# Group A's queries and gates projected with features on partitions, and the queries' norm moved into the scale of the exponential

## The chip, the cores and the metric

The kernel runs on one core of a Trainium2 chip. The metric is the time of one execution on the device in microseconds (us), the median over runs. Engines are named as in the profile: PE (TensorE, the matmuls) with PEld (its weight loads), DVE (VectorE), ACT (ScalarE), POOL (GpSimd) and SP (SyncE, which issues most transfers). Products run on float32r operands; where full precision is wanted, a tensor is split into a high and a low part and three products (high by high, high by low, low by high) are summed.

## The reference

Two layers of a trunk with 512 latent tokens and 256 context tokens, 1024 wide. A layer norms and modulates the tokens, projects them to the queries, keys and values of three groups of heads (A, B, C, eight heads of 64 features each) and to a gate, attends, multiplies by the gate and projects back. The second layer computes the latents alone. Group A, which the change touches:

```python
def rmsnorm(x, w):
    xf = x.astype(jnp.float32)
    y = xf * lax.rsqrt(jnp.mean(xf * xf, axis=-1, keepdims=True) + EPS)
    return y.astype(x.dtype) * w

def apply_rope(x, cos, sin):
    x1, x2 = jnp.split(x, 2, axis=-1)
    ...
    return jnp.concatenate([x1 * c - x2 * s, x1 * s + x2 * c], axis=-1)

def global_gqa(q, k, v, qc, kc, vc, cos, sin, qn, kn, need_ctx):
    scale = HEAD_DIM ** -0.5
    q = apply_rope(rmsnorm(heads(q, N_HEADS_A), qn), cos, sin) * scale
    k = apply_rope(rmsnorm(heads(k, N_KV_A), kn), cos, sin)
    ...
    def block(qi):
        s = jnp.einsum('bqhgd,bkhd->bhgqk', qi, k_all)
        p = softmax_f32(s, v_all.dtype)
        return jnp.einsum('bhgqk,bkhd->bqhgd', p, v_all)

# in layer():
    ux = jnp.concatenate([ya, yb, yc_], axis=-1) * jax.nn.silu(px[9])
```

The context's queries of A are normed and scaled too, not rotated, and read the context's keys only.

## The kernel before

**Layout.** The normed tokens stand with features on partitions, as `hh` and `hl` (high and low), eight tiles of 128 features: `hL` for the 512 latents, `hC` for the 256 context tokens. There are two ways to project. `proj_t` (products at L341) makes the tokens the stationary operand and streams 256 columns of weights: the result has 128 tokens on partitions; per token tile 8 x 3 = 24 products, two tiles to a PSUM bank. `proj_f` (L318) makes 128 columns of weights stationary and streams tokens: the result has features on partitions, 24 products of 512 columns for the latents and 24 of 256 for the context. Both call `done` on each finished bank. A's keys, values, queries and gates, B's values and gates went by `proj_t`; B's queries and keys and all of C by `proj_f`. The banks `pj` are two.

**A's queries before.** `a_pair` projects the queries and the gate of two heads together. For each block of two token tiles, `done` runs `rope_a` (L816): a copy `qs` on ACT (L821, where POOL does the rest), squares (L826), two products with tables of cosine and sine that hold the norm's weight (L830), a sum of the squares (L835), the inverse root as a power on POOL (L837), the rotation's addition (L839) and the norm's product (L840). Then a split (L894, L895), four transposes on PE (L899, tile `qd`) and two copies into the query tiles `qt` (L902). The gate takes a tanh on ACT (L879) and a DVE operation (L880). The table `EN` says which of POOL and DVE does what: for the first pair of A, DVE; for the others, POOL.

**C's queries**, by contrast, come with features on partitions: `rope_c` (L965) copies the result to `tA`, swaps 32-row blocks into `tB` by four transfers from ACT's queue (L978), and makes two products and an addition on POOL (L979 to L981); `c_q` splits into `qt` (L989 on ACT, L990 on POOL).

**Attention.** `GlobalUnit` (A, latents) computes scores of two query tiles into `Sbig` (L1049), a negated row maximum on DVE (L1158, tile `negm`), the exponential on ACT with it as bias (L1160, tile `P`), then transposes of `P` on PE (L1054, tile `T`), copied as high and low parts `pth` (ACT, L798) and `ptl` (DVE, L1044), and the products with V into `Obig` (L1049). `CtxUnit` does the same for context queries, `BandUnit` (C) and `NearUnit` (B) for their windows. `finish` turns the inverse sums (with the gate in them for A and B, alone for C) with PE transposes and writes the gated result `u`. Of C the gate has features on partitions, and the product with it is a pass of its own on POOL (L1354).

**Order.** `PLAN` lists stages: while one pair of heads attends, the next items are projected. In each layer the order is B0 to B3 and then A0, C0, A1, C1, A2, C2, A3, C3; A's pair i + 1 is projected during C's pair i, A's first pair during B3. `weave` interleaves the two streams and orders projections behind attention instructions; a scheduler then fixes each engine's order before the run. Every engine takes its instructions in that order, so one that waits holds all behind it. Weights arrive in `ws` by SP and are split into `wh` (ACT, L247) and `wl` (L250, POOL in the stages of A and C).

Of the kernel before, what the change touches and what calls it, by code (L numbers as in the profile page):

```python
# [19 lines left out]
D = 1024  # L20
# [35 lines left out]
SM_N = 88  # L56
BC_QN, BC_KN, BC_SINK = 0, 128, 256
BC_N = 272


EN = dict(qdk="D", q0="D", q1="P", q2="P", q3="P", cqlo="P", cklo="P", ckcp="D", cr0="P", cr1="P", cr2="P", sq="D", spl="DP", fin="P", tab="P")


def body(tc, xT, small, bcast, rpb, adaw, adat, wt, wf, wo, trigA, trigC, mskB, mskC, outT):
# [22 lines left out]
    nc.vector.memset(onesw, 1.0)  # L87
    negsink = const.tile([128, 16], F32)
# [683 lines left out]
def mixers(tc, nc, l, last, p1, ps, const, env):  # L772
    g_ = env
    en, pace = g_["en"], g_["pace"]
    (pj, Sbig, psT, psO, half_O, opv, after, ADA, wlo, proj_f, proj_t, ada, ada_load, ident, identr, bc, onesw, mhalf, negsink, udram, dram, hpool, rpb,
     trigA, trigC, mskB, mskC) = [g_[k] for k in (
         "pj", "Sbig", "psT", "psO", "half_O", "opv", "after", "ADA", "wlo", "proj_f", "proj_t", "ada", "ada_load", "ident", "identr", "bc", "onesw", "mhalf",
         "negsink", "udram", "dram", "hpool", "rpb", "trigA", "trigC", "mskB", "mskC")]
# [25 lines left out]
    def tables_a(l, j):  # L804

        base = slot("P").rearrange("p (c t f) -> p c t f", c=2, f=64)
        nc.sync.dma_start(base, trigA)
        nw = p1.tile([128, 64], F32, name="nw", bufs=1)
        off = (BC_QN, BC_KN)[j]
        nc.vector.tensor_scalar(nw, bc[:, off + l * 64:off + l * 64 + 64], 0.125 if j == 0 else 1.0, None,  # L810
                                op0=OP.mult)
        for c in range(2):
            t = tabs["qk"[j], c] = p1.tile([128, 6, 64], F32, name=f"tab{j}{c}", tag=f"tab{c}" if j else f"tabq{c}", bufs=1)
            en("tab").tensor_mul(t, base[:, c], nw[:, None, :].to_broadcast([128, 6, 64]))

    def rope_a(p, t2, j, e):  # L816

        src = p[:, :, 0:128].rearrange("p t (h f) -> p t h f", h=2)
        if e is nc.gpsimd:
            qs = p1.tile([128, 4, 64], F32, name="qs", bufs=2)  # L820
            nc.scalar.activation(qs.rearrange("p (t h) f -> p t h f", t=2), src, AF.Copy)  # L821
            src = qs.rearrange("p (t h) f -> p t h f", t=2)
# [4 lines left out]
        if e is nc.gpsimd:  # L827
            yield
        for c, t in enumerate((t1, t2_)):
            e.tensor_mul(t.rearrange("p (t h) f -> p t h f", t=2), src,  # L830
                         tabs[j, c][:, t2:t2 + 2, None, :].to_broadcast([128, 2, 2, 64]))
        if e is not nc.gpsimd:
            yield
        ss = p1.tile([128, 4], F32, name="ssA", bufs=2)
        nc.vector.tensor_reduce(ss, sq, axis=AX.X, op=OP.add)  # L835
        e.tensor_scalar(ss, ss, 1.0 / HD, EPS, op0=OP.mult, op1=OP.add)
        nc.gpsimd.tensor_tensor(ss, ss, mhalf[:, 0:4], op=OP.pow)  # L837
        t4 = [t.rearrange("p g (s f) -> p g s f", s=2) for t in (t1, t2_)]
        e.tensor_add(t4[0], t4[0], t4[1][:, :, ::-1, :])  # L839
        e.tensor_mul(t1, t1, ss[:, :, None].to_broadcast([128, 4, 64]))  # L840
        yield t1

    def a_kv(bank):
# [3 lines left out]
        def done(p, t2):  # L847
            r = rope_a(p, t2, "k", nc.vector)
# [33 lines left out]

    def a_pair(i, bank):
        Q = [newQ() for _ in range(2)]
        G = newG()

        def done(p, t2):
            e = en(f"q{i}")
            r = rope_a(p, t2, "q", e)
            next(r)  # L890
            g_silu(G, p, t2)
            t1 = next(r)
            qd = p1.tile([128, 4, 128], F32R, name="qd", bufs=2)
# [71 lines left out]
    def rope_c(s, scale, need_ctx, bank):  # L965
# [11 lines left out]
        for b in range(4):  # L977
            nc.scalar.dma_start(sw[b * 32:(b + 1) * 32], q[(b ^ 1) * 32:((b ^ 1) + 1) * 32])  # L978
# [692 lines left out]
```

## Time and profile before

| | us |
|---|---|
| median of three runs | 1199.4 |
| lowest and highest run | 1198.95, 1202.98 |
| span of the profiled execution | 1197.7 |

The page gives no time of the profiled execution beside its span. PE's clock was granted in full in every slice. A row of a group reads: line, engine, operation, out<-in, shapes and count, then the busy time and mean duration, then the idle time of the engine just before them and what ended it. Durations of matmuls overlap: the next begins before the one before has ended.

### The profile page before, as it was taken

What the parts mean: (1) busy time and instruction counts of PE and PEld (TensorE: products, weight loads), DVE (VectorE), ACT (ScalarE), POOL (GpSimd) and SP (SyncE); (2) the same over time, 40 slices, a digit from 0 to 9 for tenths busy, and PEclk for the clock granted to TensorE, in tenths of its full rate; (3) what the DMA queues carried; (4) which work ended last, traced back from release to release, by engine and by line L of the source; (5) the groups of instructions that cost most, each with busy time, mean ns of one, the idle gap of its engine ahead of it and who ended that gap; (6) DMA issues with size and microseconds to landing.
All of it is one profiled execution on the core that took longest, in us unless ns stands there. A gap on an engine that the chain in (4) does not pass through costs nothing.

```text
span 1197.7 us, 21749 instructions
## 1 busy us (share of the span) xinstructions
PE 1150.5 (96%) x8016; PEld 1034.8 (86%) x8016; DVE 769.4 (64%) x1548; ACT 696.9 (58%) x1581; POOL 408.1 (34%) x496
## 2 busy tenths in 40 slices
PE   5999999999999999999999999999999999998997
PEld 3898999998898988988778999989988888887876
DVE  5767566764656665568578895567754556567563
ACT  5446555656666676588423544555666667677552
POOL 1341110234446354385000030202274563656001
PEclk9999999999999999999999999999999999999999
DMA  9552222313312112123086662323222111232152
GB/s 321 213 142 89 78 78 67 123 66 104 111 70 92 67 44 92 34 63 119 27 293 198 205 210 74 98 84 109 91 73 67 53 46 53 63 88 72 36 161 77
DMA packets 60826, 124.22 MB, mean 104 GB/s; under 512 B 7216, under 2 KB 13488, under 8 KB 60720
## 3 DMA queue, kind: packets, MB, share of 16 engines
q1 hardware_dynamic: 54768, 111.96, 29.6%
q10 hardware_dynamic: 5952, 10.88, 2.7%
q8 instruction: 63, 1.03, 0.3%
q14 instruction: 43, 0.35, 0.1%
HBM read 109.05 MB, written 11.14 MB: 100 GB/s over the span
## 4 chain that ended last, share of the span: by engine, by line
PE 81%; DVE 5%; ACT 5%; DMA 3%; issue 3%; POOL 1%; SPq 0%; ACTq 0%; DVEq 0%; POOLq 0%
PE pj L318 18%; PE pj L341 17%; PE Sbig L1049 9%; PE Obig L1049 9%; PE T L1054 9%; PE pj L519 5%; PE T L519 3%; PE Sbig L519 3%; PE T L341 2%; PE Sbig L430 2%; DVE ptl L1044 1%; DMA x<-xT_dram 1%; PE Sbig L341 1%; ACT pth L798 1%; PE pj L430 1%
## 5 line engine op out<-in xcount | busy, mean ns | idle before, releaser
L1044 DVE TENSOR_TENSOR ptl<-T,pth 128x512 fp32r<-128x512 f32 (+2 forms) x312 | 181.1, 591 | 128.6 <-ACT pth L798 126.7
L798 ACT ACTIVATE pth<-T 128x512 fp32r<-128x512 f32 (+2 forms) x312 | 158.9, 520 | 134.8 <-PE T L1054 128.1
L341 PE MATMUL pj<-wh,hL 128*128 128x256 f32 x896 | 180.6, 287 | 0.0
L318 PE MATMUL pj<-hL,wh 128*128 128x512 f32 x544 | 175.0, 401 | 0.9 <-ACT wh L247 0.5
L1054 PE MATMUL T<-ident,P 128*128 128x128 f32 x1024 | 165.7, 273 | 4.0 <-ACT qt L902 1.7
L247 ACT ACTIVATE wh<-ws 128x512 fp32r<-128x512 f32 x192 | 119.5, 629 | 78.6 <-PE pj L318 16.3
L1049 PE MATMUL Sbig<-kt,qt 128*128 128x256 f32 (+1 forms) x864 | 156.2, 308 | 4.6 <-ACT P L1160 2.5
L250 POOL TENSOR_TENSOR wl<-ws,wh 128x512 fp32r<-128x512 f32 x76 | 98.5, 1300 | 146.4 <-ACT wh L247 146.4
L341 PEld LDWEIGHTS pj<-wh,hL 128*128 128x128 f32 x896 | 144.2, 190 | 1.0 <-issue 0.2
L1049 PE MATMUL Obig<-pth,vt 128*128 128x256 f32 (+2 forms) x432 | 134.6, 321 | 4.6 <-ACT pth L798 2.0
L1054 PEld LDWEIGHTS T<-ident,P 128*128 128x128 f32 x1024 | 123.0, 140 | 17.6 <-DVE ptl L1044 2.2
L1049 PE MATMUL Obig<-ptl,vt 128*128 128x256 f32 (+2 forms) x432 | 131.4, 318 | 5.0 <-DVE ptl L1044 4.3
L1049 PEld LDWEIGHTS Sbig<-kt,qt 128*128 128x128 f32 x864 | 123.3, 189 | 13.4 <-DVE negm L1208 4.1
L341 PE MATMUL pj<-wl,hL 128*128 128x256 f32 x448 | 128.0, 286 | 0.0
L318 PEld LDWEIGHTS pj<-hL,wh 128*128 128x128 f32 x544 | 96.2, 189 | 16.7 <-ACT wh L247 0.9
L250 DVE TENSOR_TENSOR wl<-ws,wh 128x512 fp32r<-128x512 f32 x116 | 82.7, 720 | 40.4 <-ACT wh L247 31.6
L318 PE MATMUL pj<-hL,wl 128*128 128x512 f32 x272 | 107.1, 394 | 0.5 <-DVE wl L250 0.5
L1049 PEld LDWEIGHTS Obig<-pth,vt 128*128 128x128 f32 x432 | 81.6, 189 | 15.9 <-ACT pth L798 7.1
L1049 PEld LDWEIGHTS Obig<-ptl,vt 128*128 128x128 f32 x432 | 81.5, 189 | 14.7 <-DVE ptl L1044 11.3
L1445 POOL TENSOR_TENSOR bm<-wr,bm 128x192 f32<-128x192 f32 (+1 forms) x48 | 41.3, 888 | 139.6 <-DMA bm<-mskB_dram 132.4
L341 PEld LDWEIGHTS pj<-wl,hL 128*128 128x128 f32 x448 | 85.4, 191 | 0.3
L1158 DVE TENSOR_REDUCE negm<-Sbig 128x1 f32<-128x768 f32 x64 | 61.0, 953 | 29.7 <-PE Sbig L1049 15.7
(336 smaller groups left out, 2495.6 us busy)
## 6 DMA issues: line engine op xcount, KB each, us to landing
ws<-wf_dram SPq DMA_DIRECT2D x72, 256.0 KB, 3.1
ws<-wt_dram SPq DMA_DIRECT2D x72, 256.0 KB, 3.0
ada<-adaw_dram SPq DMA_DIRECT2D x32, 512.0 KB, 5.5
ws<-wo_dram SPq DMA_DIRECT2D x57, 256.0 KB, 2.8
bm<-mskB_dram SPq DMA_DIRECT2D x16, 576.0 KB, 3.7
dw<-adat_dram SPq DMA_DIRECT2D x8, 512.0 KB, 8.2
dots<-adat_dram SPq DMA_DIRECT2D x16, 256.0 KB, 4.5
u<-u ACTq DMA_DIRECT2D x9, 384.0 KB, 2.9
```

The source lines that it names most:

```text
L247: nc.scalar.activation(hi, src, AF.Copy)
L250: eng.tensor_sub(lo, src, hi.bitcast(F32))
L318: paced(nc.tensor.matmul(p[:, 0:n], a[:, r, :], cols(b[kt], c0, n), start=(i == 0), stop=(i == 23)), i)
L341: paced(nc.tensor.matmul(p[:, t * 256:(t + 1) * 256], tok(a[kt], t2 + t), b[:, r, :], start=(i == 0), stop=(i == 23)), i)
L430: mm = nc.tensor.matmul(out, a, b, start=begin, stop=(kt == KT - 1 and i == 2), skip_group_check=True)
L519: mm = nc.tensor.matmul(p[:, 0:n], a[:, r, :], ucols(ua[b][ft], c0, n), start=(ft == FT_ORDER[0] and i == 0), stop=(ft == FT_ORDER[-1] and ...
L798: nc.scalar.activation(out, src, AF.Copy)
L1044: i = nc.vector.tensor_sub(lo[:, 0:n], T[:, 0:n], hi[:, 0:n].bitcast(F32))
L1049: m = nc.tensor.matmul(*args, **kw)
L1054: m = nc.tensor.transpose(*args, **kw)
L1158: nc.vector.tensor_reduce(nm, S, axis=AX.X, op=OP.max, negate=True)
L1445: nc.gpsimd.tensor_add(b, src, b)
```

## The change

The queries and the gates of A are projected by `proj_f`, the queries first and the gate behind them, each with features on partitions. The queries get no norm before the scores: they are copied, rotated as C's are (with tables that hold the norm's weight) and split as C's are. In the meantime their squares are split in a high and a low part, and products with a tile `pairs` of ones (two columns, one for each head of the pair) sum them over each head's features; they land in the bank of the projection itself, with tokens on partitions. A power gives `rs`, the inverse root that also holds the 1/8 of the scores. `rs` multiplies the negated maximum and is the scale of the exponential. In `finish` A goes the way of C: the inverse sums are turned alone, and the product with the gate is a pass on POOL. Both now use `u` in place of `tR` (C) or the gate's tile (A) for what is turned.

```diff
-WT_A_KV, WT_A, WT_BV, WT_BG = 0, 1, 5, 7
-WF_BQ, WF_BK, WF_CQ, WF_CK, WF_CV, WF_CG = 0, 4, 8, 12, 13, 14
+WT_A_KV, WT_BV, WT_BG = 0, 1, 3
+WF_BQ, WF_BK, WF_CQ, WF_CK, WF_CV, WF_CG, WF_AQ, WF_AG = 0, 4, 8, 12, 13, 14, 18, 22
...
+    def tables_q():
+        for c in range(2):
+            t = tabs["q", c] = p1.tile([128, NT], F32, name=f"tabq{c}", bufs=1)
+            nc.sync.dma_start(t, trigQ[c])
+            w = SM_QN + 2 * l + c
+            en("tab").tensor_scalar(t, t, sm[:, w:w + 1], None, op0=OP.mult)
...
+    def a_q(i, bank):
+        q = p1.tile([128, NT], F32, name="tA", bufs=CFG["tA"])
+        r = slot("tR")
+        rs = p1.tile([128, 6, 2], F32, name="rs", bufs=3)
+        def done(p, c0, n):
+            hi, lo = [p1.tile([128, NT], F32R, name="qd", bufs=2)[:, 0:n] for _ in range(2)]
+            sq = p1.tile([128, NT], F32, name="th", bufs=1)[:, 0:n]
+            if c0:
+                nc.scalar.activation(r[:, NT:NA], p, AF.Copy, scale=sm[:, SM_QN + 2 * l:SM_QN + 2 * l + 1])
+                nc.scalar.activation(sq, p, AF.Square)
+            else:
+                nc.scalar.activation(q, p, AF.Copy)
+                nc.vector.tensor_mul(sq, p, q)
+            nc.scalar.activation(hi, sq, AF.Copy)
+            nc.gpsimd.tensor_sub(lo, sq, hi.bitcast(F32))
+            first = None
+            for t in range(n // 128):
+                for x in (hi, lo):
+                    m = nc.tensor.matmul(p[:, 2 * t:2 * t + 2], x[:, t * 128:(t + 1) * 128], pairs, start=first is None,
+                                         stop=x is lo, skip_group_check=True)
...
+            nc.vector.tensor_scalar(v, p[:, 0:2 * k], HD * EPS, None, op0=OP.add)
+            nc.gpsimd.tensor_tensor(v, v, mhalf[:, 0:2 * k], op=OP.pow)
+        yield from proj_f(l, WF_AQ + i, need_cq, bank, done)
+        return split_q(rope(q, r, "q")), rs
+
     def a_pair(i, bank):
...
+        Q, rs = yield from a_q(i, bank)
+        G = yield from f_gate(WF_AG + i, newG(), bank)
+        return Q, G, rs
...
                 nc.vector.tensor_reduce(nm, S, axis=AX.X, op=OP.max, negate=True)
+                r = self.c["rs"][:, i, self.h:self.h + 1]
+                nc.vector.tensor_mul(nm, nm, r)
                 P = newP()
-                nc.scalar.activation(P, S, AF.Exp, bias=nm, accum_out=self.stat("sums", i))
+                nc.scalar.activation(P, S, AF.Exp, bias=nm, scale=r, accum_out=self.stat("sums", i))
...
+        R = (G if kind == "B" else u).rearrange("p (t h f) -> p t h f", h=2, f=64)
...
-            if kind == "C":
+            if kind == "B":
+                nc.vector.scalar_tensor_tensor(u[:, a:b], OT[:, a:b], 0.5, T[:, 0:b - a], op0=OP.mult, op1=OP.mult)
+            else:
                 nc.vector.scalar_tensor_tensor(OT[:, a:b], OT[:, a:b], 0.5, T[:, 0:b - a], op0=OP.mult, op1=OP.mult)
                 e = nc.vector if end else nc.gpsimd
-                if c0 == 0:
+                if kind == "C" and c0 == 0:
                     e.tensor_mul(colmajor(u[:, 0:NT]), rowmajor(OT[:, 0:NT]), colmajor(G[:, 0:NT]))
                 else:
                     e.tensor_mul(u[:, a:b], OT[:, a:b], G[:, a:b])
...
-    time = dict(akv=15.7, a=15.7 * nq / 6, ckv=15.7, c=2 * tq, b=7.8 + tq, v=15.7, g=15.7 * nq / 6)
+    time = dict(akv=15.7, a=2 * tq, ckv=15.7, c=2 * tq, b=7.8 + tq, v=15.7, g=15.7 * nq / 6)
```

`rope`, `split_q` and `f_gate` hold what `rope_c`, `c_q` and the gate of C held before; in `CtxUnit` the maximum and the scale change in the same way. The scheduler sets a new order. On PE, in layer 1, the end of the projection of A's second pair stood like this before (L318 is a projection of C, L899 the transposes of the last two query tiles, L1054 those of P, L341 the projection of A):

```order
L318 MATMUL pj<-hL,wh 128x512 x2
L318 MATMUL pj<-hL,wl 128x512
L318 MATMUL pj<-hL,wh 128x512 x2
L318 MATMUL pj<-hL,wl 128x512
L1049 MATMUL Obig<-ptl,vt 128x256
L899 MATMUL T<-identr,qd 128x128 x4
L1054 MATMUL T<-ident,P 128x128 x4
L341 MATMUL pj<-wh,hL 128x256
```

On PE, the same pair's queries in the change (L325 is the last of their projection, L1078 the transposes of P, L1073 products of the attention, L908 the sums):

```order
L325 MATMUL pj<-hL,wl 128x512
L1078 MATMUL T<-ident,P 128x128 x8
L1073 MATMUL Obig<-pth,vt 128x256
L1073 MATMUL Obig<-ptl,vt 128x256
L1073 MATMUL Obig<-pth,vt 128x256
L1073 MATMUL Obig<-ptl,vt 128x256
L1073 MATMUL Obig<-pth,vt 128x256
L1078 MATMUL T<-ident,P 128x128 x4
L908 MATMUL pj<-pairs,qd 128x2
```

The four transposes have gone; the first sum, of the high part, stands 12 transposes and 5 products behind the end of the projection, and the other seven stand eight score products, four transposes and three products further on.

On ACT, near the end of C's first pair in layer 1, after the gated result of A's first pair has been sent off (`u_0`), before:

```order
L1366 DMA u_0_11687<-u 128x512
L247 ACTIVATE wh<-ws 128x512 x2
L1211 ACTIVATE P,sums<-P,negm 128x640
L821 ACTIVATE qs<-pj 128x256
L879 ACTIVATE th<-pj 128x256
L247 ACTIVATE wh<-ws 128x512
L902 ACTIVATE qt<-T 128x256 x2
L798 ACTIVATE pth<-T 128x512
L826 ACTIVATE tA<-qs 128x256
```

and in the change (L1049 is the gate's tanh, L254 the split of weights, L805 the copies of P's transposes, L1241 C's exponentials):

```order
L254 ACTIVATE wh<-ws 128x512
L1049 ACTIVATE th<-pj 128x512
L1391 DMA u_0_11340<-u 128x512
L1241 ACTIVATE P,sums<-P,negm 128x640
L805 ACTIVATE pth<-T 128x512
L805 ACTIVATE pth<-T 128x256
L805 ACTIVATE pth<-T 128x384 x2
L1241 ACTIVATE P,sums<-P,negm 128x640
```

The queries' copies and squares no longer stand among the attention's copies here; they have moved to earlier rows, with the four transfers of the rotation.

More of the change, by code (lines that the diff above doesn't have):

```diff
@@ L774, in mixers @@
     en, pace = g_["en"], g_["pace"]
[L775 to L778, printed above, removed]
+    (pj, Sbig, psT, psO, half_O, opv, after, ADA, wlo, proj_f, proj_t, ada, ada_load, ident, identr, bc, sm, pairs, onesw, mhalf, negsink, udram, dram, hpool, rpb,
+     trigA, trigQ, trigC, mskB, mskC) = [g_[k] for k in (
+         "pj", "Sbig", "psT", "psO", "half_O", "opv", "after", "ADA", "wlo", "proj_f", "proj_t", "ada", "ada_load", "ident", "identr", "bc", "sm", "pairs", "onesw", "mhalf",
+         "negsink", "udram", "dram", "hpool", "rpb", "trigA", "trigQ", "trigC", "mskB", "mskC")]
     nq = 4 if last else 6
```

161 lines of the change are left out of this document (72 added, 89 removed).

## The prediction

> **What bounds the kernel now.** I read the page's busy line, then the chain that ended last, then a table of stretches.
>
> ```profile
> span 1197.7 us, 21749 instructions
> PE 1150.5 (96%) x8016; PEld 1034.8 (86%) x8016; DVE 769.4 (64%) x1548; ACT 696.9 (58%) x1581; POOL 408.1 (34%) x496
> PE 81%; DVE 5%; ACT 5%; DMA 3%; issue 3%; POOL 1%; SPq 0%; ACTq 0%; DVEq 0%; POOLq 0%
> ```
>
> TensorE (PE) is busy 96% of the span and carries 81% of the chain; no other engine passes 64%. So a change pays either through less work on PE, or through shorter holes in PE's stream. The changed stages are those in which a pair of heads of A or C attends while the next pair is projected. Three such periods of layer 1 (columns: stretch, length, then busy time and instructions of PE, its weight loads, DVE, ACT, POOL, then clock and DMA):
>
> ```profile
> 910.00:960.00 50.00, 47.27 (x329) 42.59 (x327) 25.90 (x54) 31.23 (x72) 27.00 (x31) 1.00 0.16 51
> 960.00:1018.00 58.00, 55.97 (x382) 50.13 (x382) 34.81 (x65) 40.01 (x90) 30.16 (x37) 1.00 0.16 51
> 1018.00:1078.00 60.00, 58.91 (x398) 52.41 (x396) 37.09 (x68) 42.43 (x94) 35.56 (x43) 1.00 0.26 75
> ```
>
> Here too PE is the fullest, at the whole granted clock, and its holes are 2.73 + 2.03 + 1.09 = 5.85 us in 168 us. That is the stock from which shorter waits can be paid in layer 1. The sum below is therefore PE's: products first, holes second.
>
> **Term 1, projections with 512 columns.** Per pair and layer the queries and gates took 24 products for each of 6 or 4 token tiles, 256 columns wide: 4 x 144 + 4 x 96 = 960. Now they are 4 x 96 = 384 products of 512 columns and 4 x 48 = 192 of 256. So 768 narrow products become 384 wide ones over the same columns. What one occupies is its share of an unbroken run in the chain, not its shown duration, since products overlap (columns: start, length, count):
>
> ```profile
> 845.25 3.23 PE pj L341 x27
> 870.65 4.58 PE pj L318 x20
> 930.23 2.78 PE pj L318 x12
> 1161.85 15.87 PE pj L519 x70
> ```
>
> 256 columns: 3.23 / 27 = 0.1196 us. 512 columns: 4.58 / 20 = 0.229, 2.78 / 12 = 0.2317, and 15.87 / 70 = 0.2267 in a long pure run. Two narrow ones cost 0.2393, a wide one 0.2293 by the middle value: 384 x 0.010 = **-3.8 us**, between 384 x 0.0076 = -2.9 and 384 x 0.0126 = -4.8.
>
> **Term 2, transposes against sums.** Gone are 80 float32r transposes of the queries (L899). New are 80 products with two columns, which sum the squares of a head. Each still loads 128 x 128 weights. The same kind of transpose in a group of four:
>
> ```profile
> 251.56 0.46 PE L860 MATMUL T<-identr,qd 128*128 128x128 f32 x4
> 251.86 0.35 PE L1049 MATMUL Obig<-ptl,vt 128*128 128x256 f32 x1
> ```
>
> Four begin within 0.30 us, 0.075 each. The profile has no float32r product of two columns. If the moving columns alone set the step, 126 columns fewer at (0.2293 - 0.1196) / 256 = 0.00043 us save 0.054 each: -4.3 us in all. From the other side stand two-column products on plain float32:
>
> ```profile
> L359 PE MATMUL Obig<-ones,sq 128*128 128x2 f32 x24 | 4.2, 289 | 0.0
> ```
>
> 4.2 / 24 = 0.175 us of busy time each would make the exchange 80 x 0.10 = +8 us. The nearest row is the float32r transpose, with the same load; I take its 0.075, so **0**.
>
> The Trainium skill, "TensorE: Matmul & The Clock Gate", section "LDWEIGHTS (loading the stationary operand)", puts a load at columns / 1.2, an estimate of 107 ns for 128 columns, and in "Back-to-back issue gap" gives a warm product a fixed 2.5 ns only. By the first the exchange would be +2.6 us, by the second term 1 would be -1.0 us. The trace has four loads and products in 0.30 us, and a fixed part of 10 ns, so I keep the rows. (What the two rules together would make of the time is the last rival.)
>
> **Term 3, waits that go.** Before, each block of two token tiles ended in a chain (copy, square, rotation, norm, split, transposes, copies) whose last block fell at the end of the projection, between the copies that the attention of C needs. Near the end of C's first pair in layer 1 (949 us) ACT ran the copy of the queries, the tanh, a weight split and two copies of transposed queries before the one on which PE waited:
>
> ```profile
> 948.73 0.36 ACT L821 ACTIVATE qs<-pj 128x256 f32<-128x256 f32 x1
> 949.00 0.37 ACT L879 ACTIVATE th<-pj 128x256 f32<-128x256 f32 x1
> 949.26 0.63 ACT L247 ACTIVATE wh<-ws 128x512 fp32r<-128x512 f32 x1
> 949.78 0.65 ACT L902 ACTIVATE qt<-T 128x256 fp32r<-128x256 f32 x2
> 950.49 0.44 PE L1054 MATMUL T<-ident,P 128*128 128x128 f32 x2 [1.15 <-ACT qt L902]
> ```
>
> 1.15 us of PE idle. In the new order the queries are projected ahead of the gate, and ACT's rows at this place hold only the gate's tanh besides the attention's own. What is late next there is the copy of P's transposes, which is the attention's own rate. I take half of the 5.85 us of holes above, **-3.0 us**, between 0 and -5.9; layer 0, with more projection work to fill in, is counted at nothing.
>
> **Term 4, the wait that comes.** The sums cannot start before the chain ACT copy, DVE square, ACT high part (and, for the low part, POOL). PE takes its instructions in order, so what is queued behind the first sum (transposes of P and products with V) waits with it, and so do ACT and DVE, which copy those. In layer 0 the next gate projection also needs the sums' bank. There are 12 such groups, 4 x 2 in layer 0 and 4 in layer 1. Prices:
>
> ```profile
> L247 ACT ACTIVATE wh<-ws 128x512 fp32r<-128x512 f32 x192 | 119.5, 629 | 78.6 <-PE pj L318 16.3 <-PE pj L341 14.0 <-PE pj L519 11.2
> L1026 DVE SCALAR_TENSOR_TENSOR gc<-th,pj 128x512 f32<-128x512 f32 x8 | 5.5, 683 | 1.9 <-ACT th L1025 1.6 <-POOL u L1354 0.2
> L250 POOL TENSOR_TENSOR wl<-ws,wh 128x512 fp32r<-128x512 f32 x76 | 98.5, 1300 | 146.4 <-ACT wh L247 146.4
> L899 PE MATMUL T<-identr,qd 128*128 128x128 f32 x80 | 9.4, 240 | 0.9 <-DVE ptl L1044 0.4 <-DVE u L1358 0.4
> 250.77 0.60 PE L1054 MATMUL T<-ident,P 128*128 128x128 f32 x4
> 251.13 0.59 PE L1049 MATMUL Sbig<-kt,qt 128*128 128x256 f32 x3
> ```
>
> 0.63 + 0.68 + 0.63 = 1.94 us to the high part, 1.30 more to the low. The thinnest cover is the one shown from layer 1: 12 transposes (0.36 us for four by the last two rows) and 5 products of 0.12 us, 1.7 us, so there 0.3 us and more is left open; elsewhere the context's 24 products (2.9 us) and more lie between. The old transposes behind a like chain left PE idle 0.9 us in 20 groups, 0.045 each, so 0.5 us for 12; fully uncovered it is 12 x 3.24 = 39 us. I take **+1.0 us**, near the row.
>
> **Term 5, the longer softmax of A.** The negated maximum is now multiplied by the query's factor before the exponential: 64 + 8 small DVE operations, each behind a reduction. The like one on a maximum, and what waits for the exponentials:
>
> ```profile
> L1124 DVE TENSOR_SCALAR negm<-negm,negsink x8: 228/304/848, 336.5 to 582.7; 128x2 f32<-128x2 f32 x8
>   PEld Sbig L1049: 2.7, 3
>   PE Sbig L1049: 2.5, 3
> 273.97 0.90 ACT L1160 ACTIVATE P<-Sbig,negm 128x768 f32<-128x768 f32 x1
> 947.92 0.82 ACT L1211 ACTIVATE P<-P,negm 128x640 f32<-128x640 f32 x1
> ```
>
> PE waited for L1160's exponential in 3 + 3 cases, so 6 x 0.3 = **+1.8 us**; all 72 exposed would be 21.9, none 0. The cover is the projection of C beside it; without it the upper end applies. The scale itself I take at nothing: C's exponential, which has a constant one, takes 0.82 us for 640 columns where A's without takes 0.90 for 768, so by proportion (0.75) a scale costs at most 0.07 us, 5 us if all 72 were exposed; one read per partition no row shows.
>
> **The other edits, at nothing.** ACT loses 20 blocks of copies and gains fewer, wider ones, but also 32 transfers that swap rows for the rotation:
>
> ```profile
> L902 ACT ACTIVATE qt<-T 128x256 fp32r<-128x256 f32 x40 | 13.1, 380 | 7.8 <-PE T L899 6.9 <-ACT tA L973 0.7
> L978 ACTq DMA_DIRECT2D tB<-tA x40: 514/550/618, 272.4 to 1070.6; - x40
> 273.05 0.39 ACT L902 ACTIVATE qt<-T 128x256 fp32r<-128x256 f32 x1 [0.67 <-ACT tA L973]
> ```
>
> A transfer takes ACT's queue 0.55 us, 8 bursts of 2.2, but activations run between them; a burst showed one hole of 0.67 us in ACT. 8 x 0.67 = 5.4 us is the upper end; the 13.1 us of copies that go cover it. POOL's passes before and, below, the like of those it gets:
>
> ```profile
> L830 POOL TENSOR_TENSOR tC<-qs,tab 128x256 f32<-128x256 f32 x15 | 11.2, 747 | 33.8 <-ACT qs L821 33.6
> L837 POOL TENSOR_TENSOR ssA<-ssA,mhalf 128x4 f32<-128x4 f32 x26 | 26.9, 1035 | 24.0 <-DVE ssA L836 23.5
> L979 POOL TENSOR_TENSOR tR<-tA,tabx 128x512 f32<-128x512 f32 x10 | 12.9, 1291 | 13.4 <-ACT tA L973 6.1 <-PE T L1054 4.0 <-PE T L1015 3.3
> L990 POOL TENSOR_TENSOR qt<-tR,qt 64x512 fp32r<-64x512 f32 x8 | 10.7, 1336 | 1.3 <-ACT qt L989 0.7
> ```
>
> A pair of layer 1 cost it two blocks of five passes of up to 0.75 us and a power of 1.04, some 9 us; now it is three passes of rotation and one low part of the squares at 1.3, two low parts of Q at 1.34, a power of 1.04 and the product by the gate at 1.3, some 10 us: with POOL at 27 to 36 us in stretches of 50 to 60, 1 us more fits. That last product comes after DVE and with the next pair's work beside it; only for A's last pair, which feeds the output projection directly, could it be late, by 1.3 us a layer. SP issues the same weight bytes and two table loads more, at the layers' starts, with B's pairs before their use.
>
> **Sum.** -3.8 + 0 - 3.0 + 1.0 + 1.8 = -4.0 us. The execution's span is 1197.7 and nothing of it lies outside that the page shows; the median of the runs is 1199.4, 1.7 above it. So 1193.7 on the span, **1195.4 us** on the median.
>
> **Rivals.**
> - *The holes close.* All 5.85 us go, a wide product takes 0.2267 (-4.8), and the added waits stay under cover: -10.7, 1188.7 us. For it: the rows at 949 us; ACT's load falls. Against: the larger part of PE's waits there is for the attention's own copies.
> - *The sums are a new stop (slower).* If POOL takes the low part behind a rotation step that waits for its transfer, or behind a weight split (1.3 us each), each of the 12 groups holds PE about 1.3 us longer: +15.6 - 4.0 + 0.4 = +12, 1211 us. It decides from about 0.35 us a group on (4.0 / 12). For it: the order shown above puts sums close behind the chain. Against: 0.045 us a group in the old chain's row.
> - *The change does not make PE's work less.* If the two-column products step like those of L359 (0.175 us), the exchange costs 8.0, more than the wide products save: -3.8 + 8.0 - 0.2 = +4.0, 1203.4 us. For it: the same two columns. Against: that row is plain float32, and half of it from the kernel's start, where PE has pauses. The Trainium skill's rule on loads, cited under term 2, points the same way.
>
> **How the numbers follow.** The forecast has chance 0.45 (its own range 1193.4 to 1200), the closing holes 0.34, the stop 0.15, no less work on PE 0.06. Half a percent is 6.0 us, about what a measurement of this kernel can tell from no change, so faster lies under 1193.4, slower above 1205.4. Faster: 0.34 and 0.04 of the forecast's edge, 0.38. Slower: 0.15. Same: 0.47. The range 1186 to 1206 takes in the closing holes with the lower end of term 2 in part, and leaves out most of the stop, some 0.2 in all; the far ends of terms 4 and 5 need cover to fail everywhere and are left out.
>
> **What would show it.** Term 1: the lines of projection with 512 columns at 0.227 to 0.232 us in the chain. Term 2: the spacing of the two-column products. Term 3: no PE idle before transposes of P at the end of C's pairs in layer 1, stretches there with less than 1 us of holes. Term 4: PE idle before the sums, put down to ACT or POOL. Term 5: PE's wait for A's exponentials. The prediction is wrong if PE's busy time falls by less than 2 us, or if the idle before the sums passes 4 us.

## The result, and the profile after

| | us |
|---|---|
| the change, median of 5 runs | 1230.6 (1230.22 to 1235.4) |
| before, median of 5 runs | 1200.67 (1198.95 to 1202.98) |
| ratio | 1.026, 95% interval 1.0239 to 1.0281 |
| span of the profiled execution, after (before) | 1228.4 (1197.7) |

The change is slower by 2.6%, about 30 us, where 4 us less was forecast. The busy line of the page of the change:

```profile
span 1228.4 us, 20917 instructions
PE 1158.6 (94%) x7632; PEld 1020.5 (83%) x7632; DVE 776.4 (63%) x1582; ACT 699.0 (57%) x1522; POOL 432.2 (35%) x462
```

PE has 384 recorded instructions fewer and is busy 8.1 us longer; its time without work rose from 47.2 (1197.7 - 1150.5) to 69.8 us. (The prediction named a fall of PE's busy time by less than 2 us as a sign of being wrong.) So the 30.7 us of span are 22.6 of holes and 8.1 of longer work. Where they lie is shown by a table of stretches, each from the first maximum of one of A's pairs to that of the next (columns as in the prediction). Before, the second pair of layer 0, the stretch from the last pair of layer 0 to the first of layer 1, the first pair of layer 1, and the last with the end:

```profile
365.00:440.90 75.90, 74.69 (x568) 68.12 (x567) 48.32 (x97) 49.91 (x120) 35.89 (x43) 1.00 0.20 67
...
518.50:887.90 369.40, 361.12 (x2423) 326.75 (x2422) 262.08 (x520) 196.47 (x443) 89.82 (x109) 1.00 0.42 130
887.90:957.90 70.00, 66.20 (x439) 58.77 (x439) 37.79 (x71) 45.29 (x98) 38.47 (x42) 1.00 0.18 58
...
1075.70:1197.70 122.00, 108.52 (x613) 91.87 (x612) 69.50 (x120) 63.30 (x126) 24.41 (x27) 0.98 0.28 85
```

The same stretches of the change:

```profile
366.60:445.90 79.30, 75.74 (x524) 66.56 (x523) 52.08 (x105) 50.65 (x111) 38.37 (x38) 1.00 0.21 68
...
526.10:903.70 377.60, 361.22 (x2342) 322.68 (x2341) 263.14 (x517) 194.88 (x433) 91.21 (x106) 0.99 0.41 127
903.70:979.00 75.30, 71.39 (x429) 62.20 (x428) 40.06 (x76) 46.66 (x93) 44.06 (x36) 1.00 0.21 64
...
1101.50:1228.40 126.90, 111.33 (x608) 92.80 (x606) 70.71 (x127) 63.05 (x122) 19.70 (x24) 0.96 0.26 81
```

3.4, 8.2, 5.3 and 4.9 us more. Of the nine such stretches of the whole span one, ahead of A's first pair, is 2.2 us shorter, one is 0.5 us longer, and the other seven are 2.6 to 8.2 us longer: the loss is spread, and no period of A's pairs gained what the forecast gave it. In the second pair of layer 0 the hole grew from 1.21 to 3.56 us. In the long stretch the holes grew by 8.1 us (8.28 to 16.38), though it is for the most part the end of layer 0 and the pairs of B in layer 1, whose work the change leaves as it was. What PE waited for, most first behind its one wait at the start of the kernel, 12.9 us before and 12.5 in the change (engine, tile and line; what it waited for; us in total, times, longest). Before:

```profile
PE Obig L1049 <- DVE ptl L1044: 4.3, 11, 0.8
PE Sbig L1049 <- ACT P L1160: 2.5, 3, 1.1
PE Obig L1049 <- ACT pth L798: 2.0, 6, 0.5
PE Obig L1049 <- DVE OT L1072: 1.9, 4, 0.7
```

And in the change, whose lines for the same work are L1068, L805 and L1096:

```profile
PE Obig L1073 <- DVE OT L1096: 5.6, 8, 1.1
PE Obig L1073 <- DVE ptl L1068: 5.0, 12, 0.6
PE Obig L1073 <- ACT pth L805: 4.9, 11, 1.3
PE T L1078 <- DVE ptl L1068: 4.9, 7, 1.1
PE Sbig L1073 <- DVE negm L1238: 4.0, 5, 1.1
PE T L1078 <- ACT P L1190: 3.4, 2, 1.8
...
PE pj L908 <- ACT qd L903: 1.3, 1, 1.3
```

Most of these are the attention's own copies and additions and the maxima of C, which the change does not touch; L1190 is the exponential of A. That they are late because something stands ahead of them on DVE or ACT, or because PE has nothing else in its order at that place, is argued from the orders; the experiments test it in part. The sums themselves (L908) stop PE for 1.3 us in one place.

### The profile page after: what moved, and what is told of

The parts are those of the page before. It is cut to its first block, busy times and chain, and to the rows that moved or that the text cites. A ratio compares the mean times of both kernels' runs of the same rounds, so it can differ in the third digit from the quotient of the medians.

```text
span 1228.4 us, 20917 instructions
## 1 busy us (share of the span) xinstructions
PE 1158.6 (94%) x7632; PEld 1020.5 (83%) x7632; DVE 776.4 (63%) x1582; ACT 699.0 (57%) x1522; POOL 432.2 (35%) x462
## 5 line engine op out<-in xcount | busy, mean ns | idle before, releaser
L325 PE MATMUL pj<-hL,wh 128*128 128x512 f32 x800 | 258.0, 400 | 1.5 <-ACT wh L254 0.5
L1068 DVE TENSOR_TENSOR ptl<-T,pth 128x512 fp32r<-128x512 f32 (+2 forms) x312 | 181.3, 591 | 111.5 <-ACT pth L805 109.4
L805 ACT ACTIVATE pth<-T 128x512 fp32r<-128x512 f32 (+2 forms) x312 | 158.4, 518 | 135.9 <-PE T L1078 124.1
L1078 PE MATMUL T<-ident,P 128*128 128x128 f32 x1024 | 169.7, 275 | 11.1 <-DVE ptl L1068 4.1
L254 ACT ACTIVATE wh<-ws 128x512 fp32r<-128x512 f32 x192 | 119.5, 629 | 87.7 <-PE pj L325 32.6
L1073 PE MATMUL Sbig<-kt,qt 128*128 128x256 f32 (+1 forms) x864 | 159.1, 312 | 7.4 <-DVE negm L1238 4.0
L325 PEld LDWEIGHTS pj<-hL,wh 128*128 128x128 f32 x800 | 142.4, 189 | 25.7 <-ACT wh L254 0.9
L325 PE MATMUL pj<-hL,wl 128*128 128x512 f32 x400 | 158.0, 395 | 0.0
L1078 PEld LDWEIGHTS T<-ident,P 128*128 128x128 f32 x1024 | 123.9, 140 | 27.4 <-DVE ptl L1068 5.9
L1073 PE MATMUL Obig<-pth,vt 128*128 128x256 f32 (+2 forms) x432 | 135.2, 323 | 11.5 <-DVE OT L1096 5.6
L1073 PEld LDWEIGHTS Sbig<-kt,qt 128*128 128x128 f32 x864 | 124.1, 191 | 18.0 <-DVE negm L1238 7.0
L1073 PE MATMUL Obig<-ptl,vt 128*128 128x256 f32 (+2 forms) x432 | 131.1, 317 | 5.5 <-DVE ptl L1068 5.0
L1073 PEld LDWEIGHTS Obig<-pth,vt 128*128 128x128 f32 x432 | 81.8, 189 | 28.2 <-ACT pth L805 16.0
L1073 PEld LDWEIGHTS Obig<-ptl,vt 128*128 128x128 f32 x432 | 81.8, 189 | 14.7 <-DVE ptl L1068 10.5
L325 PE MATMUL pj<-hC,wh 128*128 128x256 f32 x464 | 90.2, 288 | 0.0
L325 PEld LDWEIGHTS pj<-hL,wl 128*128 128x128 f32 x400 | 75.2, 188 | 15.4
L1190 ACT ACTIVATE P<-Sbig,negm,rs 128x768 f32<-128x768 f32 x64 | 63.2, 988 | 25.5 <-DVE negm L1188 19.0
L1096 DVE TENSOR_TENSOR OT<-Obig,otmp 64x512 f32<-64x512 f32 (+1 forms) x88 | 45.0, 511 | 50.0 <-ACT otmp L1095 48.7
```

Source lines behind the costliest of these rows:

```text
L254: nc.scalar.activation(hi, src, AF.Copy)
L325: paced(nc.tensor.matmul(p[:, 0:n], a[:, r, :], cols(b[kt], c0, n), start=(i == 0), stop=(i == 23)), i)
L805: nc.scalar.activation(out, src, AF.Copy)
L1068: i = nc.vector.tensor_sub(lo[:, 0:n], T[:, 0:n], hi[:, 0:n].bitcast(F32))
L1073: m = nc.tensor.matmul(*args, **kw)
L1078: m = nc.tensor.transpose(*args, **kw)
```

## Experiments

Four theories were put against each other. **L**: the multiplications of A's maxima wait for POOL, and DVE's queue and PE behind it. **Q**: the queries' new path stops PE. **R**: the scheduler redraws the order at any edit, and the order is what costs. **S**: several additions of the change each take a share. All of these runs were timed beside the kernel before, and a ratio is to it. Where a run leaves something out of the computation, its expectation says what.

### The multiplications, ordered anew

```diff
 e1
-                nc.vector.tensor_mul(nm, nm, r)
...
-                nc.scalar.activation(q, p, AF.Copy)
+                nc.scalar.activation(q, p, AF.Copy, scale=1.0 / 1024)
 e2
-                nc.vector.tensor_mul(nm, nm, r)
+                nc.vector.tensor_scalar(nm, nm, r, None, op0=OP.mult)
 e2b
-                nc.vector.tensor_mul(nm, nm, r)
+                nc.scalar.activation(nm, nm, AF.Copy, scale=r)
 e3 (in the kernel before)
+                nc.vector.tensor_mul(nm, nm, onesw[:, 0:1])
```

> The change without the 64 multiplications of A's negated maxima on the latents (the maximum goes unscaled into the exponential's bias; the latents' queries are copied with a factor of 1/1024 so that the exponentials stay finite; the 8 of the context are kept). Theory L (the multiplications: they read two SBUF operands on DVE and last until a POOL instruction beside them ends; 22.1 us in 64, mean 0.345, against 0.14 to 0.16 where POOL is idle; DVE's queue and PE behind it wait): most of the 30 us goes, 1200 to 1212 us. Theory Q (the queries' new path and the order that the scheduler sets with it hold PE; the multiplications are hidden): 1222 to 1232 us.

> The change with each multiplication as a DVE operation of one tensor by a scalar per partition (one column each, so 16 instead of 8 for the context) in place of two tensors. Theory L: such an operation has one tensor from SBUF only; if it doesn't wait for POOL its mean falls from 0.345 to 0.15 to 0.2 us and the time to 1205 to 1218 us; if it waits like the tensor form, 0.3 us or more and 1225 to 1235. Theory Q: 1225 to 1235 either way.

> The change with each multiplication on ACT, just ahead of the exponential, as a copy with a scale per partition (one column each). ACT's smallest operations take about 0.2 us, so 80 cost it some 16 us of 1228. Theory L: DVE no longer waits for POOL in this chain, 1205 to 1218 us. Theory Q: 1225 to 1240 us, as ACT gets 16 us more.

> The kernel before with 72 multiplications of A's negated maxima by a constant tile of ones, on DVE, at the place where the change has them, and nothing else. Theory L: they wait for POOL there too and make it 8 to 25 us slower, 1208 to 1225 us. Theory Q: within 4 us of before, 1198 to 1204 us.

| run | median, us | ratio to before |
|---|---|---|
| e1, no multiplication | 1225.4 | 1.0222 (1.0202 to 1.0242) |
| e2, tensor by scalar | 1234.6 | 1.029 (1.0272 to 1.0307) |
| e2b, on ACT | 1233.0 | 1.027 (1.0248 to 1.0292) |
| e3, before with multiplications | 1227.5 | 1.0229 (1.0213 to 1.0244) |

These contradict each other under L and Q alike: the change without them stays 2.2% slower, and the kernel before becomes 2.3% slower by them alone (80 in fact, as the context units of B got them too). In e2 and e2b no product of two tensors on A's maxima is left to wait for POOL, and neither is faster than the change. (On ACT each took 0.29 us, not the 0.2 that was expected.) Each edit also made the scheduler write another order: at 1,924 of the 8,016 places in PE's order another product stands in e3 than before. So the work had to be parted from the order.

### The same, with the order held

A kernel's order on every engine was written out and forced on a variant by ordering edges between neighbours, which add no wait (the loop is shortened here):

```python
for k in order[engine]:
    for y in [own[engine][k]] + added_behind.get(k, []):
        if prev is not None:
            tc.add_manual_dep(y, prev.name, NoSync, reason="order")
        prev = y
```

p1 and p3 put a multiplication by one behind each of A's reductions in the order of before, as e3 does, as a product of two tensors (p1) or of a tensor by a scalar (p3). p2 and p4 hold the change's order, without the 64 multiplications of the latents (p2) or with them as a tensor by a scalar (p4).

> The kernel before with every engine held to the order that it had, and 72 multiplications of A's negated maxima by ones, each right behind its reduction on DVE. With e3 (the same work, but ordered anew by the scheduler, 1227 us) it parts the cost of the instructions from that of the new order. Theory L (the instructions, each up to 1.3 us beside POOL): 1215 to 1230 us. Theory R (what costs is the order that the scheduler sets once these operations and their prices are in its model, not the operations): 1200 to 1210 us.

> The change with every engine held to the order that it had, and the 64 multiplications of the latents' maxima taken out of it (the queries copied with a factor of 1/1024, as in e1). Theory L: 1200 to 1212 us. Theory R: the order stays, so most of the loss stays: 1218 to 1228 us.

> As p1 (the kernel before in its own order with a multiplication by one behind each of A's reductions, 1.2% slower), but as an operation of a tensor by a scalar, one column each (80 instead of 72), which took 0.21 us in e2 whatever POOL did. Theory L (the wait for POOL, up to 1.3 us, is what p1 paid): more than half of p1's 14 us goes, 1201 to 1208 us. Theory S (one more step in the chain from the scores to the exponential is what costs, 0.16 to 0.21 us on DVE and its handover): 1210 to 1217 us.

> The whole change, computing the same, every engine held to the change's order, with the 64 multiplications of the latents' maxima as a tensor by a scalar at the same places (the 8 of the context stay). In the order of the kernel before this form took 12 of 14 us off (p1, p3). If the wait for POOL costs as much in the change's order: 1216 to 1221 us. If the other stops of that order hide it, as p2 (no multiplications at all, 1226 us) suggests: 1224 to 1230 us.

| run | order of | median, us | ratio to before |
|---|---|---|---|
| p1, two tensors | before | 1215.9 | 1.0118 (1.0101 to 1.0135) |
| p3, tensor by scalar | before | 1203.9 | 1.0019 (1.0004 to 1.0034) |
| p2, none | the change | 1225.9 | 1.0198 (1.0168 to 1.0227) |
| p4, tensor by scalar | the change | 1230.3 | 1.0232 (1.0206 to 1.0258) |

In the traces PE, ACT and POOL run the same instructions in the same order in p1 and p3 as in the kernel before, and in p2 and p4 as in the change. No run held an order and changed nothing else; for the order of before p3, with its operations, is 2 us slower (0.5 to 4 by its interval), so the holding itself costs no more than that.

In the order of before the multiplication costs 14 us as a product of two tensors and 2 us as a tensor by a scalar. The groups show why, first of p1, then of p3:

```profile
L1164 DVE TENSOR_TENSOR negm<-negm,onesw 128x1 f32<-128x1 f32 x64 | 28.7, 449 | 2.2
```

```profile
L1165 DVE TENSOR_SCALAR negm<-negm,onesw 128x1 f32<-128x1 f32 x64 | 13.7, 214 | 2.3
```

And the change's timeline shows what one such product lasts until, on DVE and then on POOL (start, length):

```profile
411.41 1.22 DVE L1151 TENSOR_TENSOR negm<-negm,rs 128x2 f32<-128x2 f32 x1
412.56 0.15 DVE L916 TENSOR_SCALAR rs<-pj 128x8 f32<-128x8 f32 x1
```

```profile
411.33 1.29 POOL L991 TENSOR_TENSOR tB<-tB,tabq 128x512 f32<-128x512 f32 x1
```

The product begins at 411.41 and ends at 412.63, 0.01 us after POOL's at 412.62; with POOL idle the same operation takes 0.14 to 0.16 us. Over the 72 of the change the time beyond 0.15 is 17 us. Of the 72, 28 took more than 0.25 us, the longest 1.75, and each of these 28 ended 0.01 to 0.02 us behind an operation of POOL. The Trainium skill, "SBUF — State Buffer", section "Who interferes with whom", says that a DVE instruction with two SBUF inputs contends with a GpSimd instruction that reads SBUF, and calls the ports that the two share an exclusive lock; the trace agrees. With a scalar operand and one column none of the 144 operations of p3 and p4 took more than 0.22 us, though 58 of them lay wholly beside an operation of POOL. Two columns are another matter: the operation on C's maxima, a tensor by a scalar on 128x2 (L1124 before), took 0.23 us twice beside an idle POOL and 0.26 to 0.85 us in its six other places, where it ended 0.02 to 0.03 us behind POOL.

How DVE's wait reaches PE is seen in p1: PE's waits for `ptl` and `OT`, which DVE writes, rise from 8.0 us before (4.3 + 1.8 + 1.9) to 16.3 (7.8 + 4.6 + 3.9), and are 10.8 in p3. So theory L is right about the mechanism and about its price in the order of before. In the change's order the price is smaller: 1.026 falls to 1.0232 without the wait in the 64 (p4; the intervals overlap, so this is not clear of noise) and to 1.0198 without the operation (p2). In the profiled executions PE's holes are 64.0 us in p4 and 64.6 in p2 against 69.8 in the change, but PE is busy 5.9 and 3.0 us longer; 5.1 and 1.7 of these are pieces at half clock, 7 and 5 where the change has 4 (the last section tells of them). That PE is often held there by something else at the same moment, so that the wait is hidden, was not shown.

### The other additions

```diff
 e4
-            nc.scalar.dma_start(sw[b * 32:(b + 1) * 32], q[...])
+            (nc.sync if tab == "q" else nc.scalar).dma_start(sw[b * 32:(b + 1) * 32], q[...])
 a1 (the squares, hi, lo, products with pairs and the powers go)
+            nc.vector.memset(rs[:, t0:t0 + k].rearrange("p t h -> p (t h)"), 1.0)
 a3 = a1 and e4, and
-                nc.vector.tensor_mul(nm, nm, r)
...
-                nc.vector.tensor_mul(nm, nm, rs[:, 4:6, self.h])
 a4 (no hi and lo; all swaps from nc.sync; tensor_scalar as in e2)
+                m = nc.tensor.matmul(p[:, 2 * t:2 * t + 2], sq[:, t * 128:(t + 1) * 128], onepair, start=first is None,
+                                     stop=True, skip_group_check=True)
```

> The change with the four transfers that swap rows of A's queries (tB) issued from SP in place of ACT; C's stay on ACT. Theory S (the loss is the sum of three additions that stand among the attention's own work on ACT and DVE: the sums with their copies, the multiplications, and these 32 issues of 0.55 us on ACT): 5 to 15 us less than the change, 1215 to 1226 us. Theory R (only the order, which any edit redraws): no lean either way, 1220 to 1240 us.

> The change without the sums of squares: no squares, no high and low parts, no products with pairs and no powers; rs is set to 1 by a memset, so the queries aren't normed. The multiplications and the scale of the exponential stay. Theory S: 8 to 18 us less than the change, 1212 to 1223 us. Theory R: 1220 to 1240 us.

> The change without all three: no sums (rs set to 1), no multiplications, and the swaps of A's queries issued from SP. What is left of the change are the wide products, the rotation, the gate and the finish with features on partitions. Theory S: all of the loss goes, 1194 to 1206 us. Theory R or Q (the projection and the finish in their new form are at fault): 1212 to 1235 us.

> The whole change, computing the same, with its three additions made cheaper: the sums as float32 products of the squares themselves (4 and 2 with two columns in place of 8 and 4; no high and low parts on ACT and POOL), the multiplication as a tensor by a scalar (0.21 us in e2), and all swaps, C's too, issued from SP. Theory S: 15 to 30 us less than the change, 1200 to 1215 us. Theory R: 1220 to 1240 us.

| run | median, us | ratio to before |
|---|---|---|
| e4, swaps of A from SP | 1231.0 | 1.0241 (1.0209 to 1.0272) |
| a1, no sums | 1225.0 | 1.0198 (1.0165 to 1.023) |
| a3, none of the three | 1215.3 | 1.0104 (1.0075 to 1.0133) |
| a4, all three made cheaper | 1224.4 | 1.0186 (1.0162 to 1.0209) |

The swaps from ACT cost nothing that can be told (1.0241 against 1.026), though e4's order too was drawn anew, which alone can move the time by some us. In the timeline of the change an issue on ACT's queue goes on beside an activation:

```profile
408.02 0.98 ACT L1190 ACTIVATE P<-Sbig,negm,rs 128x768 f32<-128x768 f32 x1
408.24 0.60 ACTq L989 DMA_DIRECT2D tB<-tA  x1
```

Without the sums the change is some 6 to 7 us faster (1.026 to 1.0198); the order was drawn anew in these runs, so that this size is not the sums' alone. Without sums and multiplications 1.0% is left, 12 us. a4 computes what the change computes and is 0.7% faster than it, in an order of its own, the best of that kind here, and still 1.9% behind the kernel before. Theory S expected 1200 to 1215 us of it and is not borne out in this size. No run beat the kernel before.

### The same work in other orders

One number of the weaving was changed, the lead of the attention over the projection that is ordered behind it: `lead=6.0` to 5.5 and to 7.0, in the kernel before (n2, b1), in the change (n6, b2) and in a3, the bare form (b4, b3).

> The kernel before with one number of the weaving changed (the lead by which attention runs ahead of the projection that is ordered behind it, 6.0 to 5.5 us), the work the same. Theory R: the kernel before stands at an order that happens to be good, and a neighbour costs 5 to 30 us: 1205 to 1230 us. Theory Q (the change's own new work and waits are at fault): within 4 us of before, 1196 to 1204 us.

> The change with the same number changed, 6.0 to 5.5 us. Theory R: orders scatter by 5 us and more, so anything from 1205 to 1240 us. Theory Q: within 4 us of the change, 1226 to 1235 us.

> The kernel before with the lead at 7.0 in place of 6.0. With n2 (5.5: 1212 us) a third order of the same work. Theory R: 1206 to 1222 us. If 6.0 to 5.5 was an exception: 1199 to 1204 us.

> The change with the lead at 7.0. If the change's own additions cost some 25 us at any order: 22 to 35 us above the kernel before at the same lead. Theory R (scatter alone): anywhere between the two known values of the kernel before and of the change, 1205 to 1235 us.

> a3 (the change without sums, multiplications and swaps from ACT; 1215 us) with the lead at 7.0. If the wide products, the rotation and the finish cost nothing by themselves and the 13 us of a3 were its order: within 5 us of the kernel before at the same lead. If the form costs: 8 to 16 us above it.

> a3 (without sums, multiplications and swaps from ACT) with the lead at 5.5, where the kernel before takes 1212 us (n2) and the change 1252 us (n6). If the projection with features on partitions costs nothing beyond its order: 1205 to 1219 us. If it costs: 1220 to 1230 us.

| lead | before | bare form | the change |
|---|---|---|---|
| 5.5 | 1212.2, ratio 1.0079 | 1220.8, 1.0162 | 1252.6, 1.0437 |
| 6.0 | 1200.7, 1 | 1215.3, 1.0104 | 1230.6, 1.026 |
| 7.0 | 1211.1, 1.0064 | 1213.9, 1.0099 | 1248.4, 1.037 |

R holds in part: the kernel before stands at a good order, and its neighbours cost 8 to 10 us at the same work. But each column keeps its place at every lead. The change lies 2.6 to 3.6 points above before at the same lead; the bare form 0.4 to 1.0, and at 7.0 the intervals of before and the bare form overlap. So the bare form gains nothing at any of three orders, and the larger part of the loss (1.6 to 2.8 points, the change against the bare form) comes with the sums and the multiplications (and the swaps, which e4 could not tell from nothing). At 7.0 and 5.5 the change lay above every range that was expected of it, and the bare form fell in the range of "costs nothing" at 7.0 and of "costs" at 5.5. Removed one by one the sums and the multiplications show 0.6 points each, the multiplications in the change's own order (p2), the sums in one drawn anew (a1).

## Why the prediction failed, point by point

- **PE is the bound, and its holes are the stock.** The first half was right: PE is still the fullest engine. The second was the step that failed: the 5.85 us of holes were read as what can be paid, down to nothing. They are also what can grow. Terms 3 to 5 together took 0.2 us off PE's holes (-3.0 + 1.0 + 1.8); the holes of all stages grew by 22.6 us, far more than the work saved. In the three periods of layer 1 from its first pair of A to its last, which were to pay, they grew from 6.62 to 11.38 us. The sum priced waits only at places where PE had waited before, as if the cover at all others would stay. A new order alone, at the same work, was worth 8 to 10 us in the kernel before (n2, b1), a new operation in the old order 14 (p1); how the 22.6 us divide between the two is not shown.
- **Term 1, wide products (-3.8).** Mechanism and size were right. Two unbroken runs of the chain of the change:

```profile
981.32 5.30 PE pj L325 x23
1040.41 5.49 PE pj L325 x24
```

  5.30 / 23 = 0.230 and 5.49 / 24 = 0.229 us, as forecast. PE's busy time does not show the gain: 5.1 of the 8.1 us by which it grew are the clock (below), and the other 3.0, where terms 1 and 2 as measured make 0.9 less, are not accounted for.
- **Term 2, sums for transposes (0).** Mis-sized. Of the changed kernel's timeline on PE:

```profile
410.25 0.92 PE L908 MATMUL pj<-pairs,qd 128*128 128x2 f32 x7
411.03 0.36 PE L1073 MATMUL Obig<-pth,vt 128*128 128x256 f32 x1
```

  Seven begin within 0.78 us, 0.111 each, where 0.075 was taken: 80 x 0.036 = +2.9 us at most, as the first of a group can take less. The Trainium skill's rule that the prediction set aside here ("TensorE: Matmul & The Clock Gate", section "LDWEIGHTS (loading the stationary operand)", an estimate of 107 ns for 128 columns) agrees with this row; the row of the transposes, from which 0.075 came, was the wrong neighbour. The row of plain float32 on the other side, 0.175, was further off.
- **Term 3, waits that go (-3.0).** Wrong in sign. At the place that was quoted (P's transposes near the end of C's first pair in layer 1) ACT's copies of queries are gone, and with them the 1.15 us. But PE now stops there for 1.14 us (at 972 us) for `pth`, the very copy of P's transposes that the prediction named as the next to be late: one wait took the place of the other. PE's waits for the copies `pth` rose from 2.0 to 4.9 us in all.
- **Term 4, the sums' own wait (+1.0).** By the prediction's own sign, PE idle before the sums, it was right: 1.3 us in one place. What the sums cost beside that wait was not in the sum: a1 points to 6 to 7 us, with its new order in it, and up to 2.9 of them are term 2; where the rest comes from (the sums' copies and squares on ACT, DVE and POOL, or the order) stays open. The rival "the sums are a new stop" was the nearest in time, on the right side with +12 us, but that is luck: its stop of 1.3 us in each of 12 groups came in one, and without the sums the change is still 2.0% slower.
- **Term 5, the multiplications (+1.8).** Mis-sized, and the largest single thing found: 14 us in the order of before (p1), of which 12 are the wait for POOL (p3), and 7 in the change's own order (p2). The row that the term was priced from carried the sign of it, 228/304/848 for an operation on 128x2: with POOL idle it took 228 and 229, and the rest was the wait for POOL. Its 0.3 was multiplied by the 6 places where PE (or its weight load) had waited for an exponential before, as if the cover of the others would stay. The sign that the prediction named, PE's wait for A's exponentials, would have missed this: it rose only from 2.5 to 3.8 us (3.4 and 0.4). The stop is on the way there. The exponentials of A before and in the change:

```profile
L1160 ACT ACTIVATE P<-Sbig,negm 128x768 f32<-128x768 f32 x64 | 57.5, 899 | 10.0 <-DVE negm L1158 7.5 <-PE T L1054 1.9
L1190 ACT ACTIVATE P<-Sbig,negm,rs 128x768 f32<-128x768 f32 x64 | 63.2, 988 | 25.5 <-DVE negm L1188 19.0 <-PE T L1078 5.4 <-PE pj L325 0.7
```

  ACT's idle time ahead of them that ended with DVE's maxima rose from 7.5 to 19.0 us. Without the multiplications in the same order (p2) it is 3.9, and PE's waits for DVE's other work fall, for `ptl` ahead of transposes from 4.9 to 3.3 and for `OT` from 5.6 to 4.5 us.
- **The scale itself (0).** It was bounded at 0.07 us a time, 5 us in all. The rows above show 0.09: 988 ns with the factor per partition against 899 without, and the same on the context's 256 columns (559 against 472). Over the 80 exponentials that is 7 us of ACT; every run of the change has it, the bare form too, and none took it out.
- **The 32 issues on ACT (0).** Not contradicted: e4 shows no gain without them, in an order of its own.
- **The half-speed clock** was not in the sum at all; it is told below. By the granted clock it takes, ahead of the last products, 6.8 us of the change's profiled execution and 1.7 of that before, so 5.1 of the 30.7 us, and 5.1 of the 8.1 by which PE's busy time grew. (The page's row of the clock before, all nines, was read as the full clock in every slice; a nine there stands for 90% or more.)

What stays open: why the bare form, with 3.8 us less work and no transposes of queries, lies 4 to 12 us above the kernel before at equal leads. A part of it is the half-speed clock: a3 has five pieces at half speed where the kernel before has one, 6.8 us of the 16.5 between the two profiled spans; at 5.5 it is five against three, at 7.0, where the two kernels are closest, three each. What PE waits for most in the layers of a3 (L1051 and L1220 are its lines for the copies `ptl` and for C's maxima):

```profile
PE Obig L1056 <- DVE ptl L1051: 9.5, 18, 1.0
PE Sbig L1056 <- DVE negm L1220: 7.1, 9, 1.3
```

Against 4.3 us for `ptl` and 1.7 for C's maxima before, it is DVE's part of the attention that comes late; that the projection in longer pieces gives less to put between was argued, not tried. Nor was the scale of the exponentials, which the bare form keeps. That two parts which show 0.6 points each come to more together is also only measured.

## What to carry to other kernels

On a kernel whose bound engine is 96% busy, price an edit by how often it can make that engine wait, not by the work that it takes off. Where a scheduler writes the order, try the edit in the old order as well as in the new one, and at two or three settings, before its parts are blamed. And don't put a small DVE operation on two SBUF tensors into a chain that PE waits for while POOL works: on one column it took up to 1.6 us (p1), with a scalar operand 0.21. On two columns the scalar operand was no way out here (0.85 us beside POOL).

## What the runs showed of the hardware that was not expected

In these traces PE's clock falls to half for pieces of 3.41 us, often behind a stop that is shorter than such a piece. Four neighbouring pieces of the change (columns: stretch, length, PE's busy time and instructions, granted clock, DMA share and rate):

```profile
561.80:565.20 3.40, 2.38 (x14) 1.00 0.71 221
565.20:568.60 3.40, 1.56 (x11) 1.00 0.50 133
568.60:572.00 3.40, 3.40 (x14) 0.50 0.63 192
572.00:575.40 3.40, 3.40 (x27) 1.00 0.38 126
```

Behind the piece with 1.84 us of idle PE runs at 0.50, and a wide product takes longer (start, length):

```profile
570.33 0.63 PE L526 MATMUL pj<-hL,wl 128*128 128x512 f32 x1
570.75 0.63 PE L526 MATMUL pj<-hL,wh 128*128 128x512 f32 x1
```

The second begins 0.42 us behind the first, where 0.229 us was measured at the full clock. PE has work for the whole piece, so an estimated 1.7 us (half of 3.41) is lost on top of the stop. Counted over the 20 traces of this study (every piece after the first 40 us that ran at the full clock): of 102 pieces in which PE was idle for 1.5 us or more, 81 were followed by one at half; of 463 with 0.6 to 1.5 us, 27; of some 6,200 with less, none. Ahead of its last products the kernel before had 1 such piece, the change 4, and the change at leads of 7.0 and 5.5 had 13 and 17, 22 and 29 us. At equal leads, before and after, the clock takes an estimated 5.1 of the 30.7 us by which the profiled spans differ at 6.0, 17 of 39.3 at 7.0 and 24 of 50.0 at 5.5. It differs between executions of one kernel too: at 5.5 the profiled one took 1262.0 us at a mean granted clock of 0.974, the other three 1250.8 to 1253.3 us at 0.984 or 0.985. So such a stop can cost about twice its length, and a part of the scatter between orders is this: e3 has 9 such pieces and p1, the same multiplications of A in the order of before, 3.

Not every operation of POOL holds DVE: in eight places a product on two tensors ran beside one of POOL's powers (`rs` or `ssA`, 128x4 or 128x8), and took 0.15 to 0.19 us.
